# Stack and output-weight splits cut into pieces, and arithmetic moved off GpSimd, in a two-layer encoder trunk

## The chip, the cores and the metric

The kernel runs on one core of one Trainium2 chip. Its five engines work from queues of their own: TensorE (PE; PEld is its weight load), VectorE (DVE), ScalarE (ACT), GpSimd (POOL) and SyncE (SP, which here only issues transfers). The metric is the device time of one execution in microseconds (us), the median of several runs.

## The reference

Two layers over 1024 tokens of width 1024, all in float32. Each layer computes:

```
h    = rms_norm(x) * (1 + scale1) + shift1
proj = h @ w_in                               # 1024 x 3232, read by two head groups
A: q, k (rotary on the first quarter), v; 4 heads, two score maps per head, block-causal mask
   weights = softmax(q0 k0) - lambda * softmax(q1 k1);  o = rms_norm(weights @ v)
B: RWKV-7: token shift, decay, a delta-rule state scan over 8 heads of 64, group norm, r*k bonus, gate
x    = x + gate1 * (concat(A, B) @ w_out)
h2   = rms_norm(x) * (1 + scale2) + shift2
x    = x + gate2 * experts(h2)                # 4 groups of 8 experts, top 1 group, top 2 experts
```

and a last rms_norm follows the second layer. The conditioning (scales, shifts, gates) comes from a 1024 x 12288 product, done in layer 0.

## The kernel before, in words

Products that must be exact to float32 are made of three float32r products: a tensor x is split into `hi`, its rounded copy, and `lo = x - hi`. For the input weights (`split_w`), attention's q and k stacks (`load_head`), and the output weights (`out_weights`), `hi` is made on ACT and `lo` on POOL.

`phase_a` does everything from the first product to the output product. Its work is written as generators ("agents") that `weave` steps by rank and by a clock of planned PE time; a step yields how much PE time it issued and how long it should rest, or the name of an event to wait for. The order so made is the priority by which the queues of the engines are filled when the program is built. On the chip each queue runs strictly in its order: an instruction that waits holds up everything behind it on its engine.

The agents that matter here:

- `firsts` / `rwkv_first`: for each of four head pairs, four quarters of 256 tokens. `chain(q)` is a row of DVE instructions (L650 to L666) that makes `arv`, `bk` and `bkb`; `products`, `turn` follow on PE. `solve` is a serial row of 2 x 31 DVE instructions per head pair (L748, L750).
- `rwkv_second` / `rwkv_back` / `rwkv_last`: the state scan in 16 units, and a group norm for every two.
- `heads` / `head_qkv`: 24 projections for q, k, v, turned on PE (L1027) and spilled to memory.
- `attention`: for each head and each of 8 row tiles, scores, maximum, exponential, combination (L1186, L1187), transposes, product with v. Before a head begins, `load_head` fetches q, k, v and makes the stacks.
- `tail`: opens and closes the memory pools of the end of the phase, calls `out_weights` for rows 4 to 7 when all heads are projected and for rows 0 to 3 when head 2 is done, and adds `out_parts`, the output product.

`load_head(h)` issues eight transfers, four ACT casts of 128x1024 (L1091, L1096) and four POOL subtractions (L1092, L1097) in one go, and the caller rests for 12 us of planned time. `out_weights` is called four times in a row: a transfer, a DVE product with the gate (L1232), an ACT cast (L1233), a POOL subtraction (L1234), each 128x1024.

Of the kernel before, what the change touches and what calls it, by code (L numbers as in the profile page):

```python
# [10 lines left out]
F32 = mybir.dt.float32  # L11
F32R = mybir.dt.float32r
# [9 lines left out]
D = 1024  # L22
# [30 lines left out]
class Trunk:  # L53
# [285 lines left out]
    def split_w(self, wp, l, i, eng=None):  # L339

        nc = self.nc
        raw = wp.tile([128, NK, 128], F32, name="wa_raw", tag="wa_raw", bufs=1)
        nc.sync.dma_start(raw, self.a["w_in"][l, i])
        hi = wp.tile([128, NK, 128], F32R, name="wa_hi", tag="wa_hi")
        lo = wp.tile([128, NK, 128], F32R, name="wa_lo", tag="wa_lo")
        (eng or nc.vector.tensor_copy)(hi, raw)  # L346
        nc.gpsimd.tensor_tensor(lo, raw, hi.bitcast(F32), op=OP.subtract)  # L347
        return hi, lo


# [68 lines left out]
    def phase_a(self, l, x_src, psum, here, there):  # L419
# [128 lines left out]
        def tail():  # L548

            def pool(stack, name, side, bufs=1):  # L550
                return stack.enter_context(self.pool(name=f"{name}{l}", bufs=bufs, side=side))

            yield "ada"
            yield "sr"
            self.stage, stk, self.atp = pool(s2, "stg", there), pool(s2, "stk0", there), pool(s2, "at", there, 2)
            self.atbufs = 1
            self.attn_consts(l, self.atp)
            self.stacks, self.stk = {}, [stk]

            sp.close()  # L560
            psum.pools.update(banks(sp, "a", pj=2, aa=1))
            ps = Banks(**banks(sb, "b", at_s=1, tp=1))
            self.add(8, self.attention(ps))
            yield "H"
            s.close()
            sb.close()
            sp.close()
            self.stack.close()
            ps.pools.update(banks(sb, "c", at_s=2, tp=2))
            self.wo, self.wo_stack = {}, ExitStack()  # L570
            wp = pool(self.wo_stack, "wO", here, 4)
            gt1 = wp.tile([128, D], F32, name="gt1", bufs=1)
            nc.sync.dma_start(gt1, self.mod_row(l, 2).partition_broadcast(128))
            stk = pool(self.wo_stack, "stk1", here)
            for k in range(4, 8):
                self.out_weights(l, k, wp, gt1, stk)
            self.stk.append(stk)
            self.atp, self.atbufs = pool(s3, "at2", here, 3), 2
            self.when["H2"] = self.clock
            self.add(7, pace(iter(()), "last"), ("B", 15))  # L580
            yield "last"
            sb.close()
            self.low.close()
            ps.pools.update(banks(s3, "d", tp=2, at_s=2, po=2))
            yield "A", 1

            s2.close()
            sf.close()
            s0.close()
            self.open_output(l, x_src, there)  # L590
            self.stage = pool(s3, "stg2", here)
            self.stk.append(pool(s3, "stk2", here))
            self.when["stk2"] = self.clock
            self.add(8.5, self.out_parts(ps, [(t, 1) for t in range(NT)] + [(t, 0) for t in range(4)], l))
            yield "A", 2

            for k in range(4):
                self.out_weights(l, k, wp, gt1, stk)
            self.when["wO"] = self.clock + 10.0

        def banks(stack, tail, **n):
            return {k: stack.enter_context(self.pool(name=f"ps{k}{tail}{l}", bufs=b, space=PSUM)) for k, b in n.items()}
# [18 lines left out]
    def rwkv_first(self, hp, rp, ep, psum, krv, l2, w_up, a_up, sp):  # L621
# [22 lines left out]
        def chain(q):  # L644
# [20 lines left out]
            nc.vector.tensor_mul(bk[:, 0], v3(ta), v3(u))  # L665
            nc.vector.tensor_mul(bk[:, 1], v3(th), v3(u))  # L666
            nc.scalar.copy(arv[:, 3], v3(v))
            for j in range(2):
                nc.gpsimd.tensor_tensor(bkb[:, j], bk[:, j], pend.to_broadcast([128, 4, 64]), op=OP.mult)
            nc.gpsimd.tensor_tensor(arv[:, 0], self.id2[:, None, :].to_broadcast([128, 4, 64]), pend.to_broadcast([128, 4, 64]), op=OP.mult)  # L670
            return arv, bkb, bk, rk

        def products(q, bk, arv, z):
# [190 lines left out]
    def rwkv_back(self, hp, q, t, pool, psum):  # L864
# [10 lines left out]
        if r == 0:  # L875
            self.bo = pool.tile([128, 4, 128], F32, name="b_bo", tag="b_bo")
            self.yh = pool.tile([128, 4, 128], F32, name="b_y", tag="b_y", bufs=2)
        bs = self.bsum[:, hp, 2 * q:2 * q + 2].rearrange("p t h -> p (t h)").unsqueeze(2).to_broadcast([128, 4, 64])
        nc.gpsimd.tensor_tensor(self.bo[:, r:r + 2].rearrange("p t (h n) -> p (t h) n", h=2), e[:, 1].rearrange("p t (h n) -> p (t h) n", h=2),
                                bs, op=OP.mult)  # L880
        hs = [slice(64 * h, 64 * h + 64) for h in range(2)]
        first = 0
# [33 lines left out]
    def rwkv_last(self, hp, half, y, bo, pool, psum):  # L916
# [11 lines left out]
        nc.vector.tensor_tensor(y3, y3, rs.unsqueeze(2).to_broadcast([128, 8, 64]), op=OP.mult)  # L928
        cs = slice(128 * hp, 128 * hp + 128)
        lnx = self.lnx  # L930
        nc.gpsimd.tensor_tensor(y, y, lnx[:, 0].unsqueeze(1).to_broadcast([128, 4, 128]), op=OP.mult)
        nc.gpsimd.tensor_tensor(bo, bo, lnx[:, 1].unsqueeze(1).to_broadcast([128, 4, 128]), op=OP.add)
        nc.gpsimd.tensor_tensor(y, y, bo, op=OP.add)

        def gate():
            ps = psum.tile([128, 4, 128], F32, name="rb_gt", tag="rb")
# [78 lines left out]
    def head_qkv(self, l, h, j, wtile, pool, psum):  # L1015
# [44 lines left out]
        for g in range(2):  # L1060
# [9 lines left out]
            self.turning += 1  # L1070
            self.add(5, turns(g, x), self.clock + self.GAP_E[0])

    def load_head(self, h):


        nc, stage = self.nc, self.stage
        keep = self.stk[max(h - 1, 0)]
        qs, ks, kl = [], [], []
        halves = [slice(0, 64), slice(64, 128)]

        def tile(n, dt=F32R):
            return keep.tile([128, T], dt, name=f"at_{n}", tag=f"at_{n}")


        for j, m, x in ((1, 0, tile("q0", F32)), (1, 1, tile("q1", F32)), (0, 0, tile("v", F32)), (0, 1, stage.tile([128, T], F32, name="st", tag="st"))):
            for r in halves:
                nc.sync.dma_start(x[r], self.heads[h, j][halves[m]])
            if j:
                ks.append(tile(f"k{m}"))
                kl.append(tile(f"l{m}"))  # L1090
                nc.scalar.copy(ks[m], x)  # L1091
                nc.gpsimd.tensor_tensor(kl[m], x, ks[m].bitcast(F32), op=OP.subtract)  # L1092
            else:
                dst = tile(f"q{m}")
                qs.append(dst)
                nc.scalar.copy(dst, x)  # L1096
                nc.gpsimd.tensor_tensor(dst[64:128], x[64:128], dst[64:128].bitcast(F32), op=OP.subtract)  # L1097
        v = tile("v", F32).rearrange("p (t n) -> p t n", n=128)
        self.stacks[h] = (qs, ks, kl, v)
        nc.sync.dma_start(v, self.heads[h, 2])  # L1100

    def attention(self, psum):

# [27 lines left out]
                yield 0.11 * x[1] + 0.11, 0.0  # L1131

        for h in range(4):
            if h not in self.stacks:
                for _ in range(2):
                    yield 0.0, rest(7)
                    yield from behind()
                yield "H", h
                if h > 1:
                    yield ("H2", "stk2")[h - 2]  # L1140
                self.load_head(h)
                yield 0.0, 12.0
            pool = self.atp
            hs = {"s": pool.tile([128, 8, 2], F32, name="at_sum", tag="at_sum"),
                  "r": pool.tile([128, 8, 2], F32, name="at_rec", tag="at_rec"),
                  "g": pool.tile([128, 8], F32, name="at_g", tag="at_g"),
                  "ss": pool.tile([128, 8], F32, name="at_ss", tag="at_ss")}
            for t in range(NT):
                p = []
                for m in range(2):  # L1150
                    p.append(self.attn_scores(h, t, m, psum, hs))
                    yield 0.11 * t + 0.11, rest(t) * (1 - m)
                yield from behind()
                self.attn_combine(h, t, p, hs)
# [62 lines left out]
        nc.scalar.dma_start(self.g_up[0:96], a["rwkv_g_up"][l])  # L1217


    def out_weights(self, l, k, wp, gate, keep):  # L1220

        nc = self.nc
        free = {0: "at_v", 1: "at_l0", 4: "at_v", 5: "at_l0", 6: "at_l1", 7: "at_k0"}
        raw = keep.tile([128, D], F32, name="wo_raw", tag=free[k]) if k in free else self.stage.tile([128, D], F32, name="wo_raw", tag="st")
        nc.sync.dma_start(raw, self.a["w_out"][l][128 * k:128 * k + 128])
        if k > 3:
            hi, lo = (wp.tile([128, D], F32R, name=f"wo_{n}", tag=f"wo_{n}") for n in ("hi", "lo"))
        else:
            names = [f"at_{n}{m}" for n in "qkl" for m in range(2)] + ["at_v", None]
            hi, lo = (self.tx.tile([128, D], F32R, name="wo_x", tag="x", bufs=1) if n is None else keep.tile([128, D], F32R, name=f"wo_{k}{n}", tag=n)  # L1230
                      for n in names[2 * k:2 * k + 2])
        nc.vector.tensor_tensor(raw, raw, gate, op=OP.mult)  # L1232
        nc.scalar.copy(hi, raw)  # L1233
        nc.gpsimd.tensor_tensor(lo, raw, hi.bitcast(F32), op=OP.subtract)  # L1234
        self.wo[k] = hi, lo

    def open_output(self, l, x_src, side):

# [735 lines left out]
```

## Time and profile before

| | |
|---|---|
| median of three runs | 2728.67 us (2727.2 to 2737.83) |
| the profiled execution | 2742.43 us, of which the span is 2740.6 us |
| mean granted TensorE clock | 0.912 of full speed |
| PE / DVE / ACT / POOL busy | 2400.2 / 1836.7 / 1131.5 / 711.9 us |

Busy time is the union of an engine's instructions, register and semaphore work left out. The clock is the share of 2.4 GHz that was granted: 1.0 is 2.4 GHz throughout, 0.5 would be 1.2 GHz throughout. Layer 0's phase runs from about 80 to 900 us, its experts from 1010 to 1385; layer 1's phase runs from about 1440 to 2200, its experts from 2325 to 2690.

### The profile page before, as it was taken

What the parts mean: (1) busy time and instruction counts of PE and PEld (TensorE: products, weight loads), DVE (VectorE), ACT (ScalarE), POOL (GpSimd) and SP (SyncE); (2) the same over time, 40 slices, a digit from 0 to 9 for tenths busy, and PEclk for the clock granted to TensorE, in tenths of its full rate; (3) what the DMA queues carried; (4) which work ended last, traced back from release to release, by engine and by line L of the source; (5) the groups of instructions that cost most, each with busy time, mean ns of one, the idle gap of its engine ahead of it and who ended that gap; (6) DMA issues with size and microseconds to landing.
All of it is one profiled execution on the core that took longest, in us unless ns stands there. A gap on an engine that the chain in (4) does not pass through costs nothing. (4 is left out here: it accounts for less than half of the span.)

```text
span 2740.6 us, 45306 instructions
## 1 busy us (share of the span) xinstructions
PE 2400.2 (88%) x17313; PEld 1836.5 (67%) x17313; DVE 1836.7 (67%) x3803; ACT 1131.5 (41%) x2020; POOL 711.9 (26%) x525
## 2 busy tenths in 40 slices
PE   5998989898979969999959888889986897999992
PEld 3676657687767866777737666667765786677771
DVE  3358875464658477877753689974648847787775
ACT  4333332244345225555544333324426422455552
POOL 4122221313141013333311222323314200233330
PEclk7999988798979979999979989889988897999996
DMA  8476675534272258999851434355426224899985
GB/s 286 159 233 222 177 218 155 155 115 132 88 218 70 96 193 303 355 336 368 309 213 47 155 107 150 113 153 156 136 76 204 73 89 180 303 384 352 335 311 200
DMA packets 262787, 542.68 MB, mean 198 GB/s; under 512 B 76376, under 2 KB 180768, under 8 KB 232608
## 3 DMA queue, kind: packets, MB, share of 16 engines
q1 hardware_dynamic: 234560, 484.61, 52.6%
q0 software_dynamic: 23376, 40.99, 4.0%
q10 hardware_dynamic: 4624, 14.06, 1.4%
q8 instruction: 142, 2.33, 0.4%
q14 instruction: 85, 0.70, 0.1%
HBM read 459.29 MB, written 120.09 MB: 211 GB/s over the span
## 5 line engine op out<-in xcount | busy, mean ns | idle before, releaser
L1618 DVE TENSOR_TENSOR w_lo<-w_gu,w_hi 128x2048 fp32r<-128x2048 f32 x134 | 306.4, 2287 | 69.1 <-ACT w_hi L1617 68.8
L1617 ACT CAST w_hi<-w_gu 128x2048 fp32r<-128x2048 f32 x134 | 255.7, 1908 | 211.0 <-PE h_ps L1670 204.3
L359 PE MATMUL pj<-hh,wa_hi 128*128 128x512 f32 x800 | 338.2, 423 | 2.1 <-DVE bsum L711 0.7
L361 PE MATMUL pj<-hh,wa_lo 128*128 128x512 f32 x800 | 328.1, 411 | 4.3 <-POOL wa_lo L347 4.3
L360 PE MATMUL pj<-hl,wa_hi 128*128 128x512 f32 x800 | 329.7, 412 | 1.2 <-DVE hl L336 1.1
L1698 POOL DMA_INDIRECT yd<-yo,idx_s x70 | 183.5, 2621 | 289.9 <-DVE yo L1695 275.1
L1709 PE MATMUL y_ps<-w_d,hT 128*128 128x512 f32 x560 | 252.3, 593 | 3.4 <-ACTq L1770 2.4
L1669 PE MATMUL h_ps<-w_hi,xT_hi 128*128 128x512 f32 x560 | 243.0, 434 | 4.4 <-ACT xT_hi L1653 4.4
L1670 PE MATMUL h_ps<-w_hi,xT_lo 128*128 128x512 f32 x560 | 222.5, 397 | 2.5 <-DVE xT_lo L1654 2.5
L1671 PE MATMUL h_ps<-w_lo,xT_hi 128*128 128x512 f32 x560 | 222.4, 397 | 0.0
L347 POOL TENSOR_TENSOR wa_lo<-wa_raw,wa_hi 128x1024 fp32r<-128x1024 f32 x50 | 123.4, 2468 | 296.2 <-ACT wa_hi L346 235.3
L359 PEld LDWEIGHTS pj<-hh,wa_hi 128*128 128x128 f32 x800 | 156.2, 195 | 42.9 <-issue 7.5
L361 PEld LDWEIGHTS pj<-hh,wa_lo 128*128 128x128 f32 x800 | 155.9, 195 | 41.1 <-POOL wa_lo L347 5.7
L360 PEld LDWEIGHTS pj<-hl,wa_hi 128*128 128x128 f32 x800 | 156.0, 195 | 37.1 <-DVE hl L336 4.4
L1709 PEld LDWEIGHTS y_ps<-w_d,hT 128*128 128x128 f32 x560 | 100.9, 190 | 104.8 <-issue 100.4
L1637 POOL DMA_INDIRECT xg<-h2d,idx_g x70 | 75.8, 1082 | 232.8 <-PE xT_ps L1645 204.2
L1669 PEld LDWEIGHTS h_ps<-w_hi,xT_hi 128*128 128x128 f32 x560 | 107.3, 192 | 38.0 <-issue 11.5
L1670 PEld LDWEIGHTS h_ps<-w_hi,xT_lo 128*128 128x128 f32 x560 | 107.3, 192 | 36.6 <-DVE th L1661 11.5
L1654 DVE TENSOR_TENSOR xT_lo<-xT_ps,xT_hi 128x1024 fp32r<-128x1024 f32 x70 | 85.7, 1225 | 65.6 <-ACT xT_hi L1653 65.6
L1671 PEld LDWEIGHTS h_ps<-w_lo,xT_hi 128*128 128x128 f32 x560 | 106.9, 191 | 23.0
L1178 ACT ACTIVATE at_p<-at_s,at_mx 128x256 f32<-128x256 f32 (+7 forms) x128 | 95.0, 743 | 64.4 <-DVE at_mx L1176 63.8
L748 DVE TENSOR_TENSOR sv_m<-sv_t,sv_n 64x31 f32<-64x31 f32 (+15 forms) x248 | 103.1, 416 | 26.4 <-DMA sv_n<-sp_z 21.8
(436 smaller groups left out, 5227.3 us busy)
## 6 DMA issues: line engine op xcount, KB each, us to landing
w_gu<-in_moe_w_gu SPq DMA_DIRECT2D x140, 1024.0 KB
w_d<-in_moe_w_down SPq DMA_DIRECT2D x70, 1024.0 KB
ada_w<-in_ada_w SPq DMA_DIRECT2D x80, 512.0 KB
wa_raw<-in_w_in SPq DMA_DIRECT2D x50, 512.0 KB
sp_z<-z SPq DMA_DIRECT2D x32, 768.0 KB
b_zz<-sp_z SPq DMA_DIRECT2D x32, 512.0 KB
cy<-yd SPq DMA_DIRECT2D x16, 1024.0 KB
qkv<-qst SPq DMA_DIRECT2D x48, 256.0 KB
```

Source lines behind the costliest of these rows:

```text
L347: nc.gpsimd.tensor_tensor(lo, raw, hi.bitcast(F32), op=OP.subtract)
L359: nc.tensor.matmul(ps, hi[:, k, :], self.hh[k][:, sl], start=(k == 0), stop=False)
L360: nc.tensor.matmul(ps, hi[:, k, :], self.hl[k][:, sl], start=False, stop=False)
L361: nc.tensor.matmul(ps, lo[:, k, :], self.hh[k][:, sl], start=False, stop=(k == NK - 1))
L748: eng.tensor_tensor(t3, tt[:, 0:j + 1, j].unsqueeze(2).to_broadcast([64, j + 1, 31 - j]), nt[:, j, j + 1:32].unsqueeze(1).to_broadcast([64 ...
L1617: self.nc.scalar.copy(hi, raw)
L1618: eng.tensor_tensor(lo, raw, hi.bitcast(F32), op=OP.subtract)
L1669: nc.tensor.matmul(ph, hi[:, k, :], whi[:, k % 4, :], start=(k == 0), stop=False)
L1670: nc.tensor.matmul(ph, lo[:, k, :], whi[:, k % 4, :], start=False, stop=False)
L1671: nc.tensor.matmul(ph, hi[:, k, :], wlo[:, k % 4, :], start=False, stop=(k == NK - 1))
L1698: st = nc.gpsimd.indirect_dma_start(out=self.yd, out_offset=bass.IndirectOffsetOnAxis(ap=self.idx_s[:, e:e + 1], axis=0), in_=yos[e % 2], ...
L1709: nc.tensor.matmul(po[:, 512 * half:512 * half + 512], hT[:, k, :], w[:, k, 512 * half:512 * half + 512], start=(k == 0), stop=(k == 1))
```

## The change

All POOL arithmetic from the first norm to the experts goes to DVE or ACT: the `lo` halves of input weights, stacks and output weights, the bonus and the affine part of the group norm go to DVE; the three products with the end-of-chunk decay in `chain` become eight ACT activations with a scale per partition. `load_head` and `out_weights` become generators: their transfers are issued first, `LAND` (4.0) us of planned time later the arithmetic begins, cut into 128x512 halves, each followed by a rest of `PIECE` (1.6) us. `load_head` becomes an agent of its own (rank 3), and `attention` waits for the event that its stacks are done. `tail` waits for head 2's stacks before it closes the pool that they are staged in.

```diff
@@ split_w
-        nc.gpsimd.tensor_tensor(lo, raw, hi.bitcast(F32), op=OP.subtract)
+        nc.vector.tensor_tensor(lo, raw, hi.bitcast(F32), op=OP.subtract)
@@ tail
-            for k in range(4, 8):
-                self.out_weights(l, k, wp, gt1, stk)
+            yield from self.out_weights(l, range(4, 8), wp, gt1, stk)
...
             yield "A", 1
+            yield "S", 2
...
-            for k in range(4):
-                self.out_weights(l, k, wp, gt1, stk)
-            self.when["wO"] = self.clock + 10.0
+            yield from self.out_weights(l, range(4), wp, gt1, stk)
+            self.when["wO"] = self.clock + 2.0
@@ rwkv_first, chain
-            for j in range(2):
-                nc.gpsimd.tensor_tensor(bkb[:, j], bk[:, j], pend.to_broadcast([128, 4, 64]), op=OP.mult)
-            nc.gpsimd.tensor_tensor(arv[:, 0], self.id2[:, None, :].to_broadcast([128, 4, 64]), pend.to_broadcast([128, 4, 64]), op=OP.mult)
+            for i in range(4):
+                nc.scalar.activation(bkb[:, :, i], bk[:, :, i], AF.Copy, scale=pend[:, i])
+            for i in range(4):
+                nc.scalar.activation(arv[:, 0, i], self.id2, AF.Copy, scale=pend[:, i])
@@ rwkv_back (bonus) and rwkv_last (lnx_g, lnx_b, sum): four instructions
-        nc.gpsimd.tensor_tensor(y, y, bo, op=OP.add)
+        nc.vector.tensor_tensor(y, y, bo, op=OP.add)
...
@@ load_head, now a generator
+        parts = []
...
             for r in halves:
                 nc.sync.dma_start(x[r], self.heads[h, j][halves[m]])
+            parts.append((j, m, x))
+        yield 0.0, self.LAND
+        for j, m, x in parts:
...
-                nc.scalar.copy(ks[m], x)
-                nc.gpsimd.tensor_tensor(kl[m], x, ks[m].bitcast(F32), op=OP.subtract)
...
+            for c in (slice(0, 512), slice(512, 1024)):
+                nc.scalar.copy(hi[:, c], x[:, c])
+                nc.vector.tensor_tensor(lo[r, c], x[r, c], hi[r, c].bitcast(F32), op=OP.subtract)
+                yield 0.0, self.PIECE
...
+        self.when["S", h] = self.clock
@@ attention
-                self.load_head(h)
-                yield 0.0, 12.0
+                self.loading.add(h)
+                self.add(3, self.load_head(h))
+            yield "S", h
...
-                    self.load_head(h + 1)
+                    self.loading.add(h + 1)
+                    self.add(3, self.load_head(h + 1))
@@ out_weights, now a generator over ks
+        raws = {k: load(k) for k in ks if k in free}
+        yield 0.0, self.LAND
+        for k in ks:
+            if k not in raws:
+                raws[k] = load(k)
+                yield 0.0, self.LAND
...
-        nc.vector.tensor_tensor(raw, raw, gate, op=OP.mult)
-        nc.scalar.copy(hi, raw)
-        nc.gpsimd.tensor_tensor(lo, raw, hi.bitcast(F32), op=OP.subtract)
+            for c in (slice(0, 512), slice(512, 1024)):
+                nc.vector.tensor_tensor(raw[:, c], raw[:, c], gate[:, c], op=OP.mult)
+                nc.scalar.copy(hi[:, c], raw[:, c])
+                nc.vector.tensor_tensor(lo[:, c], raw[:, c], hi[:, c].bitcast(F32), op=OP.subtract)
+                yield 0.0, self.PIECE
```

## Rows read from the trace of the kernel before

**Rows 1.** Stretches of the two phases: length, busy time (count) by engine, clock, DMA.

```profile
140.00:435.00 295.00, 267.41 (x2294) 193.81 (x2293) 219.35 (x535) 100.05 (x200) 76.53 (x79) 0.91 0.69 211
435.00:785.00 350.00, 312.06 (x3563) 255.02 (x3562) 198.52 (x606) 124.10 (x310) 82.91 (x61) 0.89 0.44 129
785.00:900.00 115.00, 99.02 (x550) 83.79 (x550) 85.66 (x192) 65.72 (x171) 33.98 (x21) 0.85 0.44 136
1525.00:1840.00 315.00, 271.15 (x2425) 208.45 (x2426) 252.93 (x675) 109.67 (x238) 83.32 (x74) 0.90 0.44 136
1840.00:2070.00 230.00, 202.61 (x2238) 164.36 (x2235) 120.14 (x361) 83.67 (x201) 67.74 (x45) 0.92 0.47 136
2070.00:2200.00 130.00, 104.92 (x616) 89.96 (x616) 104.73 (x216) 78.44 (x209) 34.41 (x21) 0.90 0.35 110
```

**Rows 2.** Instructions in order of time, 2056 to 2074 and 776 to 790 us.

```profile
2059.10 9.10 DVE L1232 TENSOR_TENSOR wo_raw<-wo_raw,gt 128x1024 f32<-128x1024 f32 x4 [1.61 <-DMA wo_raw<-in_w_out]
2061.48 11.24 POOL L1234 TENSOR_TENSOR wo_lo<-wo_raw,wo_hi 128x1024 fp32r<-128x1024 f32 x4 [4.72 <-ACT wo_hi L1233]
2066.21 0.80 PE L1205 MATMUL at_o<-at_v,at_wt 128*128 128x128 f32 x2 [9.19 <-ACT at_wt L1197]
2070.69 2.05 DVE L1186 SCALAR_TENSOR_TENSOR at_g<-at_sum,nlam,at_rec 128x1 f32<-128x1 f32 x1
...
779.85 0.69 PE L1196 MATMUL at_t<-ident,at_p 128*128 128x128 f32 x2 [5.09 <-ACT at_ob L1206]
786.34 3.20 DVE L1187 SCALAR_TENSOR_TENSOR at_p<-at_p,at_g,at_p 128x896 f32<-128x896 f32 x1
789.68 1.73 PE L1196 MATMUL at_t<-ident,at_p 128*128 128x128 f32 x7 [3.25 <-DVE at_p L1187]
```

**Rows 3.** The same view, 498 to 507 us and 1992 us.

```profile
498.84 1.05 ACT L1091 CAST at_k<-at_q 128x1024 fp32r<-128x1024 f32 x1 [5.50 <-DMA at_q<-qkv]
506.51 1.12 PE L1027 MATMUL qk_t<-ident,qst 128*128 128x128 f32 x4 [5.47 <-ACT qst L1069]
...
1992.59 1.97 PE L836 MATMUL rb_w<-b_e,b_tt 64*64 64x128 f32 x16 [4.80 <-ACT b_gg L861]
```

**Rows 4.** POOL's arithmetic by line: count | busy us, mean ns | idle before, releaser.

```profile
L347 POOL TENSOR_TENSOR wa_lo<-wa_raw,wa_hi 128x1024 fp32r<-128x1024 f32 x50 | 123.4, 2468 | 296.2 <-ACT wa_hi L346 235.3 <-DVE sv_t L750 23.4 <-DVE rs_u_n L107 20.9
L669 POOL TENSOR_TENSOR bkb<-bk,P 128x256 f32<-128x256 f32 x64 | 44.7, 717 | 30.1 <-PE tp L692 14.4 <-DVE bk L666 11.9 <-DVE bk L665 2.8
L1092 POOL TENSOR_TENSOR at_l<-at_q,at_k 128x1024 fp32r<-128x1024 f32 x16 | 38.9, 2433 | 56.2 <-ACT at_k L1091 56.2
L670 POOL TENSOR_TENSOR arv<-id,P 128x256 f32<-128x256 f32 x32 | 28.6, 892 | 233.8 <-PE tp L692 138.1 <-ACT P L652 38.6 <-DVE sv_t L750 18.4
L933 POOL TENSOR_TENSOR b_y<-b_y,b_bo 128x512 f32<-128x512 f32 x16 | 21.6, 1348 | 1.0
```

**Rows 5.** DVE's groups by form, whole execution.

```profile
L1186 DVE SCALAR_TENSOR_TENSOR at_g<-at_sum,nlam,at_rec 128x1 f32<-128x1 f32 x64 | 28.5, 446 | 1.3
L1232 DVE TENSOR_TENSOR wo_raw<-wo_raw,gt 128x1024 f32<-128x1024 f32 x16 | 25.6, 1618 | 6.9 <-DMA wo_raw<-in_w_out 6.8
L1212 DVE SCALAR_TENSOR_TENSOR at_ob<-at_ob,rs_y_sub,subg 128x128 f32<-128x128 f32 x64 | 24.5, 441 | 0.4
L655 DVE TENSOR_SCALAR ta<-ta 128x256 f32<-128x256 f32 x32 | 13.9, 434 | 0.6
L336 DVE TENSOR_TENSOR hl<-n_tmp,hh 128x512 fp32r<-128x512 f32 x32 | 22.1, 690 | 10.7 <-ACT hh L335 10.3
L1618 DVE TENSOR_TENSOR w_lo<-w_gu,w_hi 128x2048 fp32r<-128x2048 f32 x134 | 306.4, 2287 | 69.1 <-ACT w_hi L1617 68.8
```

**Rows 6.** DVE's groups by form, 845 to 860 us and (L655) 325 to 336 us.

```profile
L1232 DVE TENSOR_TENSOR wo_raw<-wo_raw,gt 128x1024 f32<-128x1024 f32 x2 | 2.4, 1222 | 0.4 <-DMA wo_raw<-in_w_out 0.4
L1212 DVE SCALAR_TENSOR_TENSOR at_ob<-at_ob,rs_y_sub,subg 128x128 f32<-128x128 f32 x4 | 1.1, 346 | 0.0
L1186 DVE SCALAR_TENSOR_TENSOR at_g<-at_sum,nlam,at_rec 128x1 f32<-128x1 f32 x3 | 0.7, 219 | 0.1
...
L655 DVE TENSOR_SCALAR ta<-ta 128x256 f32<-128x256 f32 x1 | 0.3, 272 | 0.0
```

**Rows 7.** ACT's groups.

```profile
L1206 ACT ACTIVATE at_ob<-at_o,at_rec 128x128 f32<-128x128 f32 x64 | 23.5, 367 | 41.2 <-PE at_o L1205 40.9
L376 ACT ACTIVATE krv<-pj,carry,omu 128x1 f32<-128x1 f32 x26 | 9.0, 346 | 0.9 <-DVE carry L373 0.8
L346 ACT CAST wa_hi<-wa_raw 128x1024 fp32r<-128x1024 f32 x46 | 48.1, 1047 | 106.8 <-PE pj L360 93.0 <-issue 7.1 <-DMA wa_raw<-in_w_in 3.7
L1091 ACT CAST at_k<-at_q 128x1024 fp32r<-128x1024 f32 x16 | 16.8, 1047 | 19.7 <-DMA at_q<-qkv 19.7
```

More of the change, by code (lines that the diff above doesn't have):

```diff
@@ L557, in tail @@
             self.attn_consts(l, self.atp)
-            self.stacks, self.stk = {}, [stk]
+            self.stacks, self.stk, self.loading = {}, [stk], set()
             sp.close()
@@ L878, in rwkv_back @@
         bs = self.bsum[:, hp, 2 * q:2 * q + 2].rearrange("p t h -> p (t h)").unsqueeze(2).to_broadcast([128, 4, 64])
-        nc.gpsimd.tensor_tensor(self.bo[:, r:r + 2].rearrange("p t (h n) -> p (t h) n", h=2), e[:, 1].rearrange("p t (h n) -> p (t h) n", h=2),
+        nc.vector.tensor_tensor(self.bo[:, r:r + 2].rearrange("p t (h n) -> p (t h) n", h=2), e[:, 1].rearrange("p t (h n) -> p (t h) n", h=2),
                                 bs, op=OP.mult)
@@ L930, in rwkv_last @@
         lnx = self.lnx
-        nc.gpsimd.tensor_tensor(y, y, lnx[:, 0].unsqueeze(1).to_broadcast([128, 4, 128]), op=OP.mult)
-        nc.gpsimd.tensor_tensor(bo, bo, lnx[:, 1].unsqueeze(1).to_broadcast([128, 4, 128]), op=OP.add)
-        nc.gpsimd.tensor_tensor(y, y, bo, op=OP.add)
+        nc.vector.tensor_tensor(y, y, lnx[:, 0].unsqueeze(1).to_broadcast([128, 4, 128]), op=OP.mult)
+        nc.vector.tensor_tensor(bo, bo, lnx[:, 1].unsqueeze(1).to_broadcast([128, 4, 128]), op=OP.add)
+        nc.vector.tensor_tensor(y, y, bo, op=OP.add)
         def gate():
@@ L1071, in head_qkv @@
             self.add(5, turns(g, x), self.clock + self.GAP_E[0])
+    LAND, PIECE = 4.0, 1.6
     def load_head(self, h):
@@ L1090, in load_head @@
                 kl.append(tile(f"l{m}"))
-                nc.scalar.copy(ks[m], x)
-                nc.gpsimd.tensor_tensor(kl[m], x, ks[m].bitcast(F32), op=OP.subtract)
-            else:
[L1094 to L1097, printed above, removed]
+                hi, lo = ks[m], kl[m]
+            else:
+                qs.append(tile(f"q{m}"))
+                hi = lo = qs[m]
+            r = slice(0, 128) if j else halves[1]
+            for c in (slice(0, 512), slice(512, 1024)):
+                nc.scalar.copy(hi[:, c], x[:, c])
+                nc.vector.tensor_tensor(lo[r, c], x[r, c], hi[r, c].bitcast(F32), op=OP.subtract)
+                yield 0.0, self.PIECE
         v = tile("v", F32).rearrange("p (t n) -> p t n", n=128)
@@ L1133, in attention @@
         for h in range(4):
-            if h not in self.stacks:
+            if h not in self.loading:
                 for _ in range(2):
@@ L1155, in attention @@
                 turn.append((h, t, p, hs))
-                if t > 1 and h < 3 and h + 1 not in self.stacks and place(h + 1):
-                    self.load_head(h + 1)
+                if t > 1 and h < 3 and h + 1 not in self.loading and place(h + 1):
+                    self.loading.add(h + 1)
+                    self.add(3, self.load_head(h + 1))
         for _ in range(2):
@@ L1217, in late_params, with out_weights, load @@
         nc.scalar.dma_start(self.g_up[0:96], a["rwkv_g_up"][l])
-    def out_weights(self, l, k, wp, gate, keep):
+    def out_weights(self, l, ks, wp, gate, keep):
         nc = self.nc
         free = {0: "at_v", 1: "at_l0", 4: "at_v", 5: "at_l0", 6: "at_l1", 7: "at_k0"}
[L1224 to L1231, printed above, removed]
-        nc.vector.tensor_tensor(raw, raw, gate, op=OP.mult)
-        nc.scalar.copy(hi, raw)
-        nc.gpsimd.tensor_tensor(lo, raw, hi.bitcast(F32), op=OP.subtract)
-        self.wo[k] = hi, lo
+        def load(k):
+            raw = keep.tile([128, D], F32, name="wo_raw", tag=free[k]) if k in free else self.stage.tile([128, D], F32, name="wo_raw", tag="st")
+            nc.sync.dma_start(raw, self.a["w_out"][l][128 * k:128 * k + 128])
+            return raw
+        raws = {k: load(k) for k in ks if k in free}
[4 more added lines that the diff above has]
+                yield 0.0, self.LAND
+            raw = raws[k]
+            if k > 3:
+                hi, lo = (wp.tile([128, D], F32R, name=f"wo_{n}", tag=f"wo_{n}") for n in ("hi", "lo"))
+            else:
+                names = [f"at_{n}{m}" for n in "qkl" for m in range(2)] + ["at_v", None]
+                hi, lo = (self.tx.tile([128, D], F32R, name="wo_x", tag="x", bufs=1) if n is None else keep.tile([128, D], F32R, name=f"wo_{k}{n}", tag=n)
+                          for n in names[2 * k:2 * k + 2])
+            for c in (slice(0, 512), slice(512, 1024)):
[3 more added lines that the diff above has]
+                yield 0.0, self.PIECE
+            self.wo[k] = hi, lo
```

## The prediction, made before the changed kernel was run

> **What bounds the kernel now.** I read the stretches of the two phases first, since the change ends before the experts. TensorE is the fullest engine in every one of them, yet it is not full: over the six stretches it stands idle 27.6 + 37.9 + 16.0 + 43.9 + 27.4 + 25.1 = 178 us, and it runs below 2.4 GHz: one minus the granted clock, times the length, adds up to 145 us [rows 1]. That is all the time that the change can touch; the experts, norms and output products outside these stretches hold no instruction of it. Two stretches have a second full engine: in the quarters (140 to 435, 1525 to 1840) DVE is busy for 219 of 295 and 253 of 315 us, and at the end of attention for 86 of 115 and 105 of 130 [rows 1]. So a stall of TensorE ends on DVE work or on work that DVE holds up, and DVE's own time counts there. In the middle stretches DVE is busy for 57% and 52%, and what is added is covered.
>
> Next I read the instructions in order of time where TensorE's waits are long. The reader sees three kinds.
>
> First, the output weights stand as one block: four gate products keep DVE for 9.10 us, and TensorE stands for 9.19 us because attention's small ACT and DVE links are behind them; in layer 0 the same block gives 5.09 us [rows 2].
>
> Second, ACT stands before a cast of `load_head` until the transfer lands, 5.50 us once, and the copies behind it, which empty TensorE's results, are late: TensorE stands for 5.47 us and, in layer 1, 4.80 us [rows 3]. ACT spends 19.7 us so on L1091 alone [rows 7].
>
> Third, DVE instructions are stretched while POOL works: `at_g`, one element per partition, takes 2.05 us, and `at_p` 3.20 us, both beside POOL's subtractions [rows 2], while `at_g` takes 0.22 us in a stretch with no POOL arithmetic [rows 6]. TensorE's 3.25 us wait stands right behind that `at_p` [rows 2].
>
> **The change part by part.** The terms are changes of the time, minus for a gain.
>
> *Output weights in halves.* The products, casts and subtractions stay, in 16 + 16 halves a layer. An attention link then waits behind one piece, about 0.69 us by the 128x512 subtraction [rows 5], and not behind 9.10 us. The three gaps are 9.19 + 5.09 + 3.25 = 17.5 us [rows 2]. The wait for the first landing (1.61 us before the block) stays. Bounds 0 and -17.5; I take -13, nearer the far end, because the blocking is seen instruction by instruction. Its place can be lost if head 2's stacks, whose buffers the raw weights occupy, come later by the rests: eight pieces at 1.6 us are 12.8 us of planned time against the 11.24 us of POOL's block [rows 2], so I put no cost on it.
>
> *Stacks as an agent.* The same eight transfers; the arithmetic is planned 4.0 us later and no longer ahead of everything. ACT's wait was up to 5.50 us beyond what had been planned, so part of it stays. Bounds 0 and -19.7 [rows 7]; TensorE's gaps show 10.3 of that [rows 3]; I take -8.
>
> *Arithmetic off POOL.* What DVE gains: four groups, whole mean against the mean away from POOL's arithmetic, give 64 x (446 - 219) + 16 x (1618 - 1222) + 64 x (441 - 346) + 32 x (434 - 272) ns = 14.5 + 6.3 + 6.1 + 5.2 = 32 us [rows 5, 6]. That is the lower bound. For the upper one: in the block of 11.24 us of POOL, DVE lost 9.10 - 4 x 1.22 = 4.2 us and 2.05 - 0.22 = 1.8 us, 0.54 of POOL's time [rows 2, 6]; times POOL's 379 us in the six stretches [rows 1] this is 205 us. I take an estimate of 110 us, near the middle, as the four groups are a small part of DVE's work there.
>
> What DVE gets: 50 input weights at 1.22 us = 61; stacks 64 halves and output weights 32 halves at 0.69 = 66; the gate in halves, 32 x 0.69 - 16 x 1.22 = 2.5; the affine parts 48 x 0.69 = 33; the bonus, 32 of 128x256, between 0.27 and 0.69 us each [rows 5, 6], at 0.4 = 13. Sum 176 us, or a net +66 on DVE (-29 to +144 by the bounds), against 1435 - 981 = 454 us in which DVE is idle [rows 1]. So DVE does not become the bound by its total; the place decides:
>
> - End of attention. The links are serial, so what `at_g` and `at_ob` lose, 14.5 + 6.1 = 20.6 us, lies on the path; the new pieces stand between them on a DVE that has 29 and 25 us left [rows 1]. I take half: -10 (0 to -20.6).
> - Quarters. POOL's share there is (76.5 + 83.3) / 379 = 0.42, so DVE is relieved of 46 us; half of the input weights, 25 x 1.22 = 31 us, come on. Net -15, half of it on the path: -8 (0 to -23).
> - Middle. +0: the affine parts and bonus are hidden by DVE's idle time; if that cover were gone, 46 us.
>
> *Decay products on ACT.* Eight activations a quarter: 128 elements with a scale per partition at 0.367, 64 elements at 0.346 or less, so 2.85 us, against 2 x 0.717 + 0.892 = 2.33 on POOL [rows 4, 7]. 32 quarters add 91 us to an ACT busy for 100 of 295 and 110 of 315 us. They are hidden by the products that TensorE does before it turns `bkb`; without that cover 32 x 0.52 = 17 us. I take +5.
>
> *New waits.* DVE now stands before a `lo` until ACT's cast is done, and everything behind it (the solve, the chain, the state adds) stands too. Where DVE already does this, it loses 69.1 / 134 = 0.52 us an instruction in the experts and 10.7 / 32 = 0.33 in the norm [rows 5]. For the 25 in the quarters 0.5 us gives 13, half on the path: +6. Elsewhere the idle time covers it.
>
> *Clock.* Terms so far: -13 - 8 - 10 - 8 + 5 + 6 = -28. Where TensorE stands less it is granted more: 145 us below full clock go with 178 us of idle [rows 1], so 28 us less idle would give 23 in proportion; some of that clock time is not on the path, so I take -15 (0 to -23).
>
> **Sum: -43 us**, that is 2742.4 - 43 = 2699 for an execution like the profiled one. That one stands 13.8 us above the median, and I carry the difference over to the median: 2728.7 - 43 = **2686 us**.
>
> On the third kind of wait the row shows `at_g` at 446 ns against 219 [rows 5, 6]. The Trainium skill, SBUF — State Buffer, "Who interferes with whom", says that DVE and GpSimd share one pair of ports under a lock held for a whole instruction, against any DVE instruction with two SBUF inputs. The traces agree in that a one-element instruction loses up to 1.8 us; the rule's full price would be the larger relief in the second case below.
>
> **The rivals.** A chance of 0.53 goes to the forecast, with its own range 2655 to 2714.
>
> *The gain is larger (0.17).* POOL blocks DVE for 0.54 of its time throughout, and the stalls go entirely: -17.5 - 19.7 - 20.6 - 23 - clock 23 + 5 = -99, **2630 us**. For it: every long DVE instruction in rows 2 stands beside POOL. Against: new DVE work takes the same place.
>
> *The stalls only move (0.16).* The pieces do not help because the first one still waits for the same landing, and DVE's relief is spent on what it takes over: the load, end and quarter terms vanish and -13 + 5 + 6 - 3 is left, about **2724 us**. For it: TensorE's own waits on POOL's results are small, its long waits name ACT and DVE. Against: the block of 9.10 us is gone whatever else happens.
>
> *Slower (0.14): DVE queues behind ACT's casts.* POOL stood 235.3 us waiting for `wa_hi` [rows 4]; that was free on POOL and is not on DVE. ACT itself waits 93.0 / 46 = 2.0 us a cast for TensorE to release the buffer [rows 7]. If DVE inherits 2.0 us for the 25 in the quarters, 50 us, and the ACT products lose their cover (12 us more), the time is 2728.7 - 43 + 50 + 12 = **2748 us**. It decides from a mean wait of (43 - 12) / 25 = 1.2 us. Against: DVE is behind in the quarters, so the cast is mostly done when it comes.
>
> **How the numbers follow.** The forecast is the likeliest case. A time is told from no change by 0.5%, 13.6 us. Faster is the first two cases, 0.70; the moved stalls are same, 0.16; slower 0.14. The range leaves out the lower half of the larger gain and the upper part of the slower case: 2634 to 2742.
>
> **What would show each step.** Right: POOL has no arithmetic from 80 to 900 and 1440 to 2200 us; `at_g` and L655 have their short means throughout; DVE's busy time in the six stretches rises by some 66 us (by 150 if the relief is small); TensorE's gaps over 4 us at the output weights and loads are gone; the clock of 785 to 900 and of 2070 to 2200 is above 0.90. Wrong: DVE's idle time before L347 is over 1.2 us an instruction, with TensorE waiting for `z`, `bk` or `arv` behind it; or ACT stands before the new activations while L371, L375 or L1069 are due and TensorE waits for its result banks. The prediction falls, too, if head 2's stacks come so late that TensorE stands between two heads.

## The result and the profile after

The changed kernel takes 2687.88 us (2685.36 to 2693.68, four runs) against 2731.43 us (2727.2 to 2737.83) for the kernel before, measured beside it: a ratio of 0.9842, 95% interval 0.9814 to 0.9869, a gain of 43.5 us. The profiled execution of after took 2686.03 us (span 2684.2 us, mean granted clock 0.926); the one of before, 2742.43 us. Those two differ by 56.4 us, of which 11 are the distance of that execution of before from its median and 2 that of the one of after from its own.

Where those 56.4 us lie is read from the last instruction of each stage in the two traces, in us:

| stage, read to | layer 0, before, after | layer 1, before, after |
|---|---|---|
| start, to the first input product | 47.3, 44.3 (-3.0) | |
| quarters, to the last product `aa` | 392.0, 385.4 (-6.6) | 368.9, 356.6 (-12.3) |
| middle, to the last `qk_t` | 333.5, 323.9 (-9.6) | 269.5, 264.3 (-5.2) |
| end of attention, to the last `at_o` | 121.7, 124.8 (+3.1) | 146.8, 128.8 (-18.0) |
| all behind it, to the next layer's first product or DVE's last instruction | 522.8, 519.5 (-3.3) | 534.3, 532.8 (-1.5) |

In this execution the gain is spread: 19 us in the quarters, 15 in the middle, 15 at the end of attention. The view by stretches of after answers to [rows 1]; layer 1 comes earlier, so its three stretches are cut earlier.

```profile
140.00:435.00 295.00, 271.64 (x2403) 201.65 (x2396) 202.80 (x559) 135.53 (x335) 8.70 (x16) 0.92 0.70 215
435.00:785.00 350.00, 302.91 (x3426) 245.18 (x3426) 223.88 (x670) 125.76 (x321) 2.62 (x11) 0.88 0.45 136
785.00:900.00 115.00, 106.04 (x638) 90.10 (x637) 87.76 (x227) 64.04 (x178) 1.62 (x3) 0.97 0.41 129
1500.00:1810.00 310.00, 279.91 (x2543) 215.45 (x2543) 244.29 (x719) 144.31 (x370) 3.50 (x7) 0.92 0.47 145
1810.00:2030.00 220.00, 192.86 (x2138) 155.26 (x2137) 136.89 (x406) 84.40 (x207) 1.28 (x7) 0.95 0.47 135
2030.00:2150.00 120.00, 107.81 (x649) 91.84 (x649) 100.30 (x255) 82.64 (x228) 0.96 (x2) 0.91 0.42 127
```

POOL (the last busy time) has next to nothing left. DVE, which took over its work, is no busier than before in the quarters: 203 against 219 us in the first row, 244 of 310 against 253 of 315 in the fourth. The groups of DVE's instructions, by shape, say why; they answer to [rows 5]:

```profile
L347 DVE TENSOR_TENSOR wa_lo<-wa_raw,wa_hi 128x1024 fp32r<-128x1024 f32 x50 | 61.0, 1220 | 44.3 <-ACT wa_hi L346 43.8 <-PE pj L361 0.2
L1104 DVE TENSOR_TENSOR at_l<-at_q,at_k 128x512 fp32r<-128x512 f32 x32 | 21.3, 684 | 14.2 <-ACT at_k L1103 14.0
L1256 DVE TENSOR_TENSOR wo_raw<-wo_raw,gt 128x512 f32<-128x512 f32 x32 | 20.6, 685 | 3.3 <-DMA wo_raw<-in_w_out 3.2
L1223 DVE SCALAR_TENSOR_TENSOR at_ob<-at_ob,rs_y_sub,subg 128x128 f32<-128x128 f32 x64 | 18.3, 347 | 0.4
L1197 DVE SCALAR_TENSOR_TENSOR at_g<-at_sum,nlam,at_rec 128x1 f32<-128x1 f32 x64 | 13.8, 216 | 0.9
L933 DVE TENSOR_TENSOR b_y<-b_y,b_bo 128x512 f32<-128x512 f32 x16 | 11.0, 689 | 0.4
L654 DVE TENSOR_SCALAR ta<-ta 128x256 f32<-128x256 f32 x32 | 9.1, 283 | 0.7
```

`at_g` fell from 446 to 216 ns, `at_ob` from 441 to 347, `ta` from 434 to 283: about the means that stood in the stretches without POOL's arithmetic [rows 6]. The new work on DVE (61.0 for the input weights, 42.6 for the stacks, 21.2 for the output weights, 33.1 for the affine parts, 12.3 for the bonus) is 170 us, and the page's DVE total rose only from 1836.7 to 1848.7 us. So DVE was relieved of 170 - 12 = 158 us.

The groups of ACT, answering to [rows 7]:

```profile
L346 ACT CAST wa_hi<-wa_raw 128x1024 fp32r<-128x1024 f32 x46 | 48.1, 1046 | 76.7 <-PE pj L360 72.5 <-DMA lam_v<-in_attn_lambda 2.4 <-DMA wa_raw<-in_w_in 1.6
L668 ACT ACTIVATE bkb<-bk,P 128x128 f32<-128x128 f32 x128 | 40.9, 395 | 2.1 <-DVE bk L664 2.1
L670 ACT ACTIVATE arv<-id,P 128x64 f32<-128x64 f32 x128 | 34.1, 339 | 0.0
L1103 ACT CAST at_k<-at_q 128x512 fp32r<-128x512 f32 x32 | 18.4, 616 | 28.9 <-DMA at_q<-qkv 26.9 <-DVE wo_lo L1258 1.9
```

The eight new activations take 395 and 339 ns and wait for almost nothing. The last row is a miss: ACT's wait for the stacks to land did not shrink, it grew from 19.7 to 26.9 us.

Nor did the block of output weights in layer 1 go. In order of time, DVE and then TensorE:

```profile
2020.55 1.29 DVE L1256 TENSOR_TENSOR wo_raw<-wo_raw,gt 128x512 f32<-128x512 f32 x2 [1.06 <-DMA wo_raw<-in_w_out]
...
2026.75 1.29 DVE L1256 TENSOR_TENSOR wo_raw<-wo_raw,gt 128x512 f32<-128x512 f32 x2
2027.95 0.62 DVE L1187 TENSOR_REDUCE at_mx<-at_s 128x1 f32<-128x128 f32 x2
...
2029.10 0.58 PE L1182 MATMUL at_s<-at_k,at_q 128*128 128x256 f32 x1 [8.46 <-ACT at_p L1189]
```

All eight gate products and four of the subtractions stand ahead of attention's maximum, and TensorE stands for 8.46 us where it stood for 9.19 [rows 2]. The planned rests order the list; when the queues were filled, the pieces came together again. In layer 0 the gate products stand close together too (755.6 to 763.9 us), but TensorE's longest wait behind them is short, where it stood for 5.09 and 3.25 us [rows 2]:

```profile
769.31 0.88 PE L1207 MATMUL at_t<-ident,at_p 128*128 128x128 f32 x3 [2.82 <-DVE at_p L1198]
```

### The profile page after: what moved, and what is told of

Same layout as the page of the kernel before. It is cut to its first block, busy times and chain, and to the rows that moved or that the text cites. A ratio compares the mean times of both kernels' runs of the same rounds, so it can differ in the third digit from the quotient of the medians.

```text
span 2684.2 us, 45428 instructions
## 1 busy us (share of the span) xinstructions
PE 2370.9 (88%) x17313; PEld 1812.1 (68%) x17313; DVE 1848.7 (69%) x4045; ACT 1200.7 (45%) x2324; POOL 313.9 (12%) x251
## 5 line engine op out<-in xcount | busy, mean ns | idle before, releaser
L359 PE MATMUL pj<-hh,wa_hi 128*128 128x512 f32 x800 | 332.5, 416 | 3.4 <-ACT wa_hi L346 3.1
L361 PE MATMUL pj<-hh,wa_lo 128*128 128x512 f32 x800 | 322.7, 405 | 3.7 <-DVE wa_lo L347 3.6
L1720 DVE SCALAR_TENSOR_TENSOR yo<-y_ps,wsl,gt 128x1024 f32<-128x1024 f32 x70 | 89.9, 1284 | 38.3 <-PE y_ps L1734 38.3
L1187 DVE TENSOR_REDUCE at_mx<-at_s 128x1 f32<-128x256 f32 (+7 forms) x128 | 95.9, 753 | 17.6 <-PE at_s L1185 16.4
L238 PE MATMUL ada_ps<-ada_w,crep 128*32 128x128 f32 x1536 | 70.2, 310 | 41.0 <-DMA ada_w<-in_ada_w 40.9
```

Of the source, the lines that this page charges most:

```text
L359: nc.tensor.matmul(ps, hi[:, k, :], self.hh[k][:, sl], start=(k == 0), stop=False)
L361: nc.tensor.matmul(ps, lo[:, k, :], self.hh[k][:, sl], start=False, stop=(k == NK - 1))
L1187: nc.vector.tensor_reduce(mx, ps[:, 0:n], axis=AX.X, op=OP.max, negate=True)
```

## Experiments

Each kernel was timed in five rounds beside the kernel before; the ratio is to the kernel before as measured beside it (2732.1, 2733.6 and 2732.0 us for the three groups of runs). "Pieces" are the cuts, rests and agents of stacks and output weights; "engines" is the arithmetic leaving GpSimd.

### Engines without pieces, pieces without engines

```diff
@@ e1_engines: the kernel before, with
-        nc.gpsimd.tensor_tensor(lo, raw, hi.bitcast(F32), op=OP.subtract)
+        nc.vector.tensor_tensor(lo, raw, hi.bitcast(F32), op=OP.subtract)
... (the same for stacks, output weights, bonus, affine parts; decay products on ACT as in the change)
@@ e2_pieces: the kernel after, with all of these lines as they were before
```

> The kernel before with all arithmetic off GpSimd and nothing cut into pieces. Theory A (the prediction: blocks and loads are worth about half, -13 - 8 and their share of the clock): -15 us against before, 0.994. Theory B (the trace of after shows the output-weight pieces still back to back in layer 1 and ACT's wait for the landings no shorter, so the gain is GpSimd's port and its latency alone): -36 to -45 us, 0.984 to 0.987.

> The kernel after with all arithmetic back on GpSimd, pieces and agents kept. Theory A: -28 us against before, 0.990. Theory B: within 8 us of before, 0.997 to 1.003; the means of at_g and L655 stay long as in before.

The engines alone: 2688.32 us, ratio 0.9825 (0.9798 to 0.9852). The pieces alone: 2745.33 us, ratio 1.0057 (1.0037 to 1.0077). The whole gain is from the engines; the cuts and rests alone are 13 us of loss, no more than what a new order of the queues moves (below). With whole pieces of 128x1024 the gaps at the output weights are 5.03 and 6.43 us in layer 0 and 7.62 in layer 1, together no shorter than before, and the kernel is as fast as after all the same:

```profile
775.25 0.69 PE L1197 MATMUL at_t<-ident,at_p 128*128 128x128 f32 x2 [5.03 <-ACT at_ob L1207]
786.88 1.73 PE L1197 MATMUL at_t<-ident,at_p 128*128 128x128 f32 x7 [6.43 <-DVE at_rec L1186]
...
2034.35 0.80 PE L1206 MATMUL at_o<-at_v,at_wt 128*128 128x128 f32 x2 [7.62 <-ACT at_wt L1198]
```

Read by the ends of its stages as in the table above, e1_engines gains 17 us in the quarters, loses 3 in the middle (606.0 against 603.0) and gains 32 at the end of attention. So how the gain is divided between the last two goes with the order of the queues; their sum, 29 or 30 us, is the same in both kernels.

### Two parts undone

```diff
@@ e3_decay_pool: the kernel after, with the three decay products on GpSimd as before
@@ e4_split_pool: the kernel after, with
-        nc.vector.tensor_tensor(lo, raw, hi.bitcast(F32), op=OP.subtract)
+        nc.gpsimd.tensor_tensor(lo, raw, hi.bitcast(F32), op=OP.subtract)
         return hi, lo
```

> The kernel after with the three decay products of a quarter back on GpSimd. Theory A (ACT pays +5, the port's stretch in the quarters is half on the path): about the time of after, 0.982 to 0.986. Theory B (in the quarters every stretch of DVE counts, and 73 us of GpSimd come back there): +8 to +15 us against after, 0.987 to 0.990.

> The kernel after with the lo halves of the input weights (123 us of GpSimd) back on GpSimd. DVE loses 61 us of work and 44 us of waiting for ACT's casts, and gets GpSimd's stretch of about 0.4 x 123 = 50 us. Theory A (the new waits cost +6 on the path): 0 to +5 us against after, 0.984 to 0.986. Theory B: +10 to +20 us, 0.988 to 0.992.

Decay products back: 2717.52 us, 0.9932 (0.9909 to 0.9954). Input weights back: 2732.18 us, 0.9989 (0.997 to 1.0007). Either takes back more than expected, and together (30 + 44 us) more than the gain of 44. So the parts do not add up, and two readings were left: the price is what DVE loses beside GpSimd, or it is that TensorE gets `lo` later.

### A ghost on GpSimd, and three parts alone

```diff
@@ g1_ghost: the kernel after, split_w
         nc.vector.tensor_tensor(lo, raw, hi.bitcast(F32), op=OP.subtract)
+        nc.gpsimd.tensor_tensor(raw, raw, hi.bitcast(F32), op=OP.subtract)
@@ d1_split: the kernel before, only split_w's subtraction on DVE
@@ d2_decay: the kernel before, only the decay products on ACT
@@ d3_rest: the kernel before, only stacks, output weights, bonus, affine parts on DVE
```

> The changed kernel, in which GpSimd also makes the 50 input-weight subtractions of before once more, in place into the raw tile, where nothing reads the result; only the next load of that tile waits for it. Theory P (what DVE loses while GpSimd works is the price): 50 x 2.47 us of GpSimd's work stand beside DVE again, and DVE keeps its own 61 us, so at least the 44 us that this subtraction cost on GpSimd come back: 2728 us or more. Theory L (what cost was that TensorE got the low halves later): nothing waits for these, so 2688 to 2695 us.

> The kernel before with the input-weight subtraction alone on DVE. Theory P, in proportion to GpSimd's time taken away (123 of 379 us): a third of the gain of 44 us, 2717 us. Theory L: nearly the whole gain, 2690 us, as undoing this part alone gave it all back. Theory N (the parts only pay together, since any one that stays keeps the links late): 2725 to 2735 us.

> The kernel before with the three decay products alone as eight ACT activations. Theory P, by GpSimd's time (73 of 379 us): 8 us of gain, 2724 us. Theory L: the 30 us that undoing it cost, 2702 us. Theory N: 2725 to 2735 us.

> The kernel before with the stacks, the output weights, the bonus and the affine part of the group norm on DVE, in whole 128x1024 pieces, and with input weights and decay products left on GpSimd. Theory P, by GpSimd's time (183 of 379 us): 21 us of gain, 2711 us, and most of it at the end of attention, where at_g falls to 0.22 us. Theory L: no gain, 2728 to 2735 us. Theory N: 2725 to 2735 us.

The ghost: 2732.79 us, 0.9998 (0.9982 to 1.0014). Subtractions whose result nobody reads give back the whole gain, as much as the real ones do in e4_split_pool; that TensorE gets `lo` late is not the price. Nor is it that the raw tile comes free later for its next load: TensorE stands idle for 4.2 us in all before the products with the input weights here, for 8.6 in after. The page's DVE total is 1908.7 us, 60.0 more than after with the same instructions, beside this GpSimd group:

```profile
L348 POOL TENSOR_TENSOR wa_raw<-wa_raw,wa_hi 128x1024 f32<-128x1024 f32 x50 | 123.5, 2471 | 842.2 <-DVE wa_lo L347 593.8 <-DVE b_sb L896 90.9 <-issue 54.5
```

How DVE loses that time is seen in the ghost's instructions in order of time:

```profile
495.20 2.35 POOL L348 TENSOR_TENSOR wa_raw<-wa_raw,wa_hi 128x1024 f32<-128x1024 f32 x1 [59.26 <-DVE wa_lo L347]
496.01 0.42 DVE L839 COPY b_w<-rb_w 128x256 f32<-128x256 f32 x1 [0.45 <-PE rb_w L837]
...
1640.61 2.35 POOL L348 TENSOR_TENSOR wa_raw<-wa_raw,wa_hi 128x1024 f32<-128x1024 f32 x1 [18.52 <-DVE wa_lo L347]
1640.73 2.38 DVE L650 TENSOR_SCALAR th<-th 128x256 f32<-128x256 f32 x1 [0.20 <-ACT th L641]
...
1879.57 2.40 DVE L1198 SCALAR_TENSOR_TENSOR at_g<-at_sum,nlam,at_rec 128x1 f32<-128x1 f32 x1
1879.60 2.36 POOL L348 TENSOR_TENSOR wa_raw<-wa_raw,wa_hi 128x1024 f32<-128x1024 f32 x1 [1.33 <-issue]
```

`at_g`, one element per partition, lasts 2.40 us and ends at 1881.97, with POOL's instruction at 1881.96. `th`, with one input, ends 0.15 us after its neighbour. The copy at 496.01 reads TensorE's result bank and takes its usual 0.42 us in the middle of POOL's subtraction. So DVE is not slowed in proportion: some of its instructions are held until GpSimd's ends, others not at all.

Where this costs time is seen by the ends of the stages. The ghost and after need 736.1 and 742.0 us for the quarters of both layers, 637.6 and 588.2 for the middle, 252.6 and 253.6 for the end of attention; e4_split_pool has 745.4, 628.5 and 252.5. The two middle stretches of the ghost, then those of after, in the columns of [rows 1]:

```profile
422.90:769.80 346.90, 298.09 (x3401) 242.63 (x3401) 207.21 (x616) 104.52 (x269) 19.81 (x17) 0.85 0.40 116
1775.30:2066.00 290.70, 253.37 (x2696) 205.83 (x2696) 179.74 (x510) 95.16 (x232) 21.17 (x17) 0.89 0.41 120
...
429.70:753.60 323.90, 286.23 (x3375) 232.06 (x3372) 194.42 (x608) 103.47 (x266) 2.59 (x10) 0.90 0.42 124
1754.50:2018.80 264.30, 240.61 (x2669) 193.04 (x2668) 164.32 (x504) 94.16 (x231) 1.64 (x9) 0.95 0.44 127
```

In the middle DVE is busy 28 us longer, TensorE stands 25 us longer, and it needs 25 us more for its products at a lower clock. In the quarters DVE is busy 28 us longer too, and TensorE does not pay. So the price was paid where DVE has the most idle time, not where it is fullest; why, and how much of it is the order's, is not shown.

The parts alone: input weights 2726.86 us, 0.9971 (0.9957 to 0.9986); decay products 2733.81, 1.0003 (0.9989 to 1.0016); the rest 2735.11, 1.0009 (0.9992 to 1.0026). Of the theories only N fits all three (d3_rest lies 0.1 us above its range): of 44 us, the three parts alone give 7, 0 and 0. d3_rest frees attention of POOL almost wholly (`at_g` 244 ns) and gains nothing in total; the 200 us of subtractions and decay products that it leaves on POOL stand in the quarters and the middle.

### A ghost that reads nothing, and other orders

Each edit makes the planner fill the queues anew, so a part of every difference may be the order's. Four kernels in which GpSimd does no arithmetic that reads test that.

```diff
@@ c1_memset: the kernel after, split_w
         nc.vector.tensor_tensor(lo, raw, hi.bitcast(F32), op=OP.subtract)
+        nc.gpsimd.memset(raw, 0.0)
@@ r1_norest: the kernel after
-    LAND, PIECE = 4.0, 1.6
+    LAND, PIECE = 0.0, 0.0
@@ r2_land8: the kernel after
+    LAND, PIECE = 8.0, 1.6
@@ i1_links: the kernel after, out_weights (self.link: attention's last maximum or combination)
+                with self.tc.issue_after(self.link.ins):
+                    nc.vector.tensor_tensor(raw[:, c], raw[:, c], gate[:, c], op=OP.mult)
```

> The changed kernel, in which GpSimd writes zeros into the raw tile of an input weight after its subtraction, 50 times, at the place where the earlier run repeated the subtraction there; nothing reads the zeros. It takes the same place in the queues and holds the same tile, but reads no operand. Theory P (the price is what DVE loses while GpSimd reads two operands): DVE's instructions keep their short means and the time stays at 2688, up to 2700 us. Theory Q (one more GpSimd instruction in the list makes the planner and the queues order the work differently, and that is the price): about 2730 us as in the run with the repeated subtraction, with DVE's busy time as in the changed kernel.

> The changed kernel with LAND and PIECE at 0: the same transfers, pieces and engines, but no planned rests, so the order of the queues is made anew with nothing on GpSimd. Theory P: it stays near the changed kernel, 2680 to 2700 us, since no instruction is stretched in any order. Theory Q: an order made anew moves the time by some 20 us a layer, either way, so it may lie anywhere from 2660 to 2730 us. The prediction's own step (stacks and weights as resting agents worth 21 us): 2709 us.

> The changed kernel with LAND at 8.0 in place of 4.0: the arithmetic behind the loads is planned 4 us later. ACT's waits for the stacks to land (26.9 us on the first two casts) should fall to under 15 us. Theory P: 2678 to 2693 us, a gain of at most the 10 us that TensorE stood behind them. Theory Q: anywhere from 2660 to 2730 us.

> The changed kernel with every gate product of the output weights put behind the last of attention's maxima and combinations that had been listed by then, on DVE's queue. In layer 0 the pieces then stand between those links, in layer 1 only part of them, since few links are listed there by then. Theory P: TensorE's gap of 8.46 us at the output weights of layer 1 shrinks, 2678 to 2688 us. Theory Q: anywhere from 2660 to 2730 us.

The write-only ghost: 2704.1 us, 0.9897 (0.9861 to 0.9932), between the two expectations. DVE's total is 1852.7 us, 4.0 above after, though GpSimd works 50 x 0.96 us at the same place. `at_g` beside it:

```profile
1637.32 0.96 POOL L348 MEMSET wa_raw<- 128x1024 f32 x1 [21.71 <-DVE wa_lo L347]
1637.52 0.90 DVE L650 TENSOR_SCALAR th<-th 128x256 f32<-128x256 f32 x1
...
1865.23 0.96 POOL L348 MEMSET wa_raw<- 128x1024 f32 x1 [1.89 <-issue]
1865.23 0.22 DVE L1198 SCALAR_TENSOR_TENSOR at_g<-at_sum,nlam,at_rec 128x1 f32<-128x1 f32 x1
```

The memset follows the same subtraction, and `at_g` takes 0.22 us beside it in place of 2.40. `th` is held by the memset too (0.90 us). The memsets are also shorter than the subtractions, 48 us in all against 123, so the totals alone do not separate reading from length; `at_g`, not held for any of the 0.96 us, does for this instruction.

The new orders: no rests 2702.0 us, 0.9889 (0.9867 to 0.9911); LAND 8.0 2712.62, 0.993 (0.9906 to 0.9954); pieces behind attention's links 2702.9, 0.9899 (0.9878 to 0.9919). All three lie outside the ranges of Theory P and inside those of Theory Q. So an order made anew, with the same instructions, moved the time by 14 to 25 us here, all of them to the slower side of after; what the moved rests and places themselves are worth cannot be told from the order. LAND 8.0 did not do what it was meant to: ACT's wait on the stacks grew to 31.5 us, where under 15 was expected. And i1_links left the gap in layer 1, where attention has hardly a link listed between those pieces:

```profile
2039.41 0.58 PE L1182 MATMUL at_s<-at_k,at_q 128*128 128x256 f32 x1 [7.90 <-ACT at_p L1189]
```

Of all the runs none beats the changed kernel; e1_engines equals it.

### All runs together

TensorE's idle time is the page's span less its PE total; "reads" is POOL's TENSOR_TENSOR time summed over the trace.

| kernel | us | reads, us | DVE total | TensorE idle |
|---|---|---|---|---|
| before | 2731 to 2734 | 403 | 1836.7 | 340 |
| e2_pieces | 2745.33 | 414 | 1841.7 | 348 |
| d2_decay | 2733.81 | 330 | 1817.5 | 346 |
| d1_split | 2726.86 | 290 | 1846.6 | 335 |
| d3_rest | 2735.11 | 200 | 1878.1 | 346 |
| g1_ghost | 2732.79 | 123 | 1908.7 | 336 |
| e4_split_pool | 2732.18 | 123 | 1857.0 | 338 |
| e3_decay_pool | 2717.52 | 87 | 1877.4 | 324 |
| r2_land8 | 2712.62 | 0 | 1849.9 | 318 |
| c1_memset | 2704.1 | 0 | 1852.7 | 311 |
| i1_links | 2702.9 | 0 | 1850.6 | 321 |
| r1_norest | 2702.0 | 0 | 1851.3 | 326 |
| e1_engines | 2688.32 | 0 | 1845.2 | 316 |
| after | 2687.88 | 0 | 1848.7 | 313 |

The medians of the two groups do not overlap: with reads 2717 to 2745 us (mean 2732), without 2688 to 2713 (mean 2700). Their nearest members, e3_decay_pool and r2_land8, cannot be told apart (0.9932 and 0.993). The difference of the means, 32 us, is an estimate of what GpSimd's reads cost whatever the order; the other 11 or so of the 43.5 us are within what the order alone moves. Inside the first group the time hardly follows the amount of reads.

## Why the prediction came out right, and where its steps did not

The time, 2686 us forecast and 2687.88 measured, is right, and the mechanism that carries it is named in the third kind of wait. That the sum came out within 2 us is in good part luck: two groups of terms were mis-sized against each other. Without the clock, the pieces were to give 21 us and gave nothing; the arithmetic with its new costs was to give 7 (-10 - 8 + 5 + 6) and brought the whole fall of TensorE's idle time, 24 us in e1_engines and 27 in after.

**Output weights in halves (-13) and stacks as an agent (-8): failed.** The pieces alone are 13 us slower than before, the engines alone are as fast as both together. What failed is "An attention link then waits behind one piece": in layer 1 the trace shows the pieces in one block again (8.46 us), and ACT's landing wait at 26.9 us in place of a smaller one. Nor do the runs show these gaps to be worth their length: in layer 0 they did shrink in after, and e1_engines, which keeps all of them, is as fast. The rival *the stalls only move* said that the pieces do not help ("the first one still waits for the same landing") and was right there, though its sum still counts the -13; it was wrong that DVE's relief is spent too.

**Arithmetic off POOL (-10, -8 and 0): right in kind, far too small.** It carries the whole gain. DVE's relief was 158 us, inside 32 to 205 but nearly half as much again as the 110 taken; with 170 us of new work (176 forecast) DVE's net is +12 where +66 was forecast. The quarters gained 19 us (-8, plus 5 and 6 for the new costs), the middle and the end of attention together 30 (0 and -10, besides the 21 for the pieces). "Middle. +0" failed, and its reason, that DVE's idle time hides what happens there: DVE is idle for over 40% of the middle [rows 1], and the ghost, whose DVE instructions are all in after as well, pays its 49 us just there. That TensorE was then waiting for one of the held instructions is the likely reason; it is not shown instruction by instruction.

**Decay products on ACT (+5): not measured by itself.** The activations wait for almost nothing (2.1 us in 128 of `bkb`). Putting the products back on GpSimd costs 30 us, but that brings GpSimd's reads back with them; moving them alone gives nothing. What ACT's longer time costs is not separated from what GpSimd's leaving gives.

**New waits (+6).** DVE stands 0.89 us before each `lo` (44.3 / 50), over the 0.5 assumed and under the 1.2 from which the slower rival decides. Nothing shows that they cost time: g1_ghost keeps them and the 61 us of subtractions on DVE, e4_split_pool has neither, both have the same 50 subtractions on GpSimd, and their times are 2732.79 and 2732.18 us.

**Clock (-15): about right.** From the pages of the two profiled executions, TensorE's idle time fell by 340.4 - 313.3 = 27.1 us, about the -28 of the terms, and its busy time by 2400.2 - 2370.9 = 29.3 us for the same 17313 products at a granted clock of 0.926 in place of 0.912. The execution of before that was profiled lies 11 us above its median, so part of the 29 us is its own. TensorE's busy time times the clock is 2189 and 2195 us on the two pages; the other executions of before had a median clock of 0.917, those of after a mean of 0.924, and by these the difference is some 18 us, an estimate. The proportion from which the term was taken is not in the rows, though: of the six stretches the one that stood idle most, 25.1 of 130 us, had 0.90, and one with 16.0 of 115 had 0.85 [rows 1]. In c1_memset the idle time is as low as in after and the busy time 24 us longer at 0.917; why its clock is lower was not tested. Two of its six executions, at 0.923 and 0.925, took 2691.2 and 2692.0 us, near those of after.

**Of the larger gain (2630 us)** one premise holds: in the groups shown, the stretching goes entirely. Its price does not, since it added the load stalls, which stayed, and the full clock.

**Not settled:** why the first 90 to 120 us of GpSimd's reads cost 30 to 45 us and the next 280 nothing more. The planner orders each kernel anew, so the same queues with more and fewer reads could not be compared.

## What to carry to other kernels

Price each GpSimd instruction that reads SBUF as a possible stop, until its end, of a DVE instruction that reads SBUF beside it, and do so also where DVE has idle time. Do not expect the price to follow the amount: taking off a fifth to a half of the reads gave 0 to 7 us here, putting 87 or 123 us of them back cost 30 to 45. GpSimd's writes without reads cost DVE 4.0 us in 50, so they can stay near short DVE links; why the kernel with them still took 16 us more than after was not found. Where a planner fills the queues, time two or three orders that change nothing else before a gain of 10 to 20 us is given to an edit; here they lay 25 us apart.

## What was not expected of the hardware

A one-element DVE instruction with its inputs in SBUF was held for 2.40 us beside a GpSimd subtraction and took 0.22 us beside a GpSimd memset; a DVE copy out of TensorE's result bank took its 0.42 us beside the same subtraction. The Trainium skill, SBUF — State Buffer, "Who interferes with whom", says that a DVE instruction with two SBUF inputs contends with GpSimd's reads and not with one that only writes; these rows agree. The same section of the Trainium skill says that tensor_scalar can enter a mode that uses both pairs of ports. `th`, a tensor_scalar, was held by the read (2.38 us) and the memset (0.90 us) alike, where its longest time in after is 0.30 us; which mode it ran in, no row shows.
